# Weights staged in half-unit tiles, and two units split behind x at the end of the first PLE

## The chip, the cores and the metric

The program runs on 1 core of one Trainium2 chip. The metric is the device time of one execution in microseconds (us); the median of several executions is compared. One execution was also taken with the hardware profiler, and all rows below are of that one. The engines are PE (TensorE, matmuls), DVE (VectorE), ACT (ScalarE), POOL (GpSimd) and SP (SyncE, which here only issues DMAs). Each works through its own instructions in their order.

## The reference, cut to what matters

A decoder trunk of two layers over 256 tokens of width 1024, in float32:

```python
for i in range(2):
    x = layer_norm(a * x + 0.5 * swiglu(x, w_gate[i, 0], w_up[i, 0], w_down[i, 0]), ...)   # 2816 hidden columns
    mix = mixer_ab(x, ...) if i % 2 == 0 else mixer_cd(x, ...)      # [Mamba-2 SSD | S5], [HGRN2 | GLA]
    x = layer_norm(a * x + mix, ...)
    x = layer_norm(a * x + 0.5 * swiglu(x, w_gate[i, 1], w_up[i, 1], w_down[i, 1]), ...)
    x = x + sigmoid(x @ ple_w_gate[i]) * (p[i] @ ple_w_proj[i])     # "PLE"
```

The stages follow each other, in the kernel's names: f00 (the first SwiGLU), LN, ab, LN, f01, LN, PLE 0, f10, LN, cd, LN, f11, LN, PLE 1. Every matrix product reads all its weights from HBM once.

## The kernel before

**Weights.** All weights lie in one array `wall` of 189 units of [128, 2048] float32 (1 MB), in the order of use. `Weights.unit()` (lines 45 to 66) fetches the next one: SP issues its load (line 53) into a staging tile `wst_n`, of which the pool has two; then for each half j of 1024 columns ACT makes the rounded copy `wh_n_j` (line 61) and DVE the remainder `wl_n_j` = staged - `wh` (line 62). PE computes each product in three matmuls, x high with `wh`, x high with `wl`, and x low with `wh` (`mm3`). A staging tile is free for the next load once the DVE subtraction of its second half is done. `wh` and `wl` live in six half-unit buffers each, which is three units; the last two down units of a SwiGLU use a pool of their own.

**x.** `split_xT` (lines 105 to 114) does the same to x, which PE has transposed into PSUM (`tp_...`): ACT writes `xh` (line 112), DVE `xl` (line 113). It keeps both instructions as `g.anchors`. x is split in four pieces, token tile t (0, 1) by half c (0, 1) of its 1024 columns.

**Order.** A scheduler orders the instructions of each engine ahead of time, by times that it works out itself. `behind` adds an order to it: an instruction may not be placed ahead of given anchors on the same engine. `layer_norm` uses it: behind a layer norm the splits of units `at+1` and `at+2` (the second and third unit of the next stage) come after the splits of x of token tiles 0 and 1. `ple` (its `finish`, lines 291 to 312) makes the new x without such an order; its x is split at once for the next stage, f10, whose first units are 99, 100 and 101.

**A SwiGLU** has 11 blocks f of 256 hidden columns. A block's gate and up products take two units (`gu_f`, 48 matmuls of 512 columns), then `hidden` applies silu and the product (`sg`, ACT line 211, DVE line 212), PE transposes (`ht`), ACT and DVE split (`hh`, `hl`, line 218), and `down` takes one unit into the four accumulators `acc` (token tile by half, 24 matmuls). PE has matmuls of the next block between.

**S5 tables in f00.** Between the blocks of f00 the engines also build the tables of the S5 mixer, in eight parts b, and store them to HBM: DVE and ACT write `s5pk_b` (one buffer; lines 516, 530, 541), PE transposes `s5w_b_0`, `s5w_b_1` and multiplies `s5k_b`, ACT copies these into `s5pe` (one buffer; lines 553, 560, 565). POOL's queue stores them to `s5d` (line 543 for `s5pk`, line 566 for `s5pe`), so the next part's copies wait until the store has landed. In the middle POOL's queue also loads `s5m_1` (line 446), the input of parts 4 to 7.

Of the kernel before, what the change touches and what calls it, by code (L numbers as in the profile page):

```python
# [8 lines left out]
F32 = mybir.dt.float32  # L9
# [3 lines left out]
ALU = mybir.AluOpType  # L13
# [4 lines left out]
P = 128  # L18
# [15 lines left out]
def f32(ap):  # L34
    return ap.bitcast(F32)


class Weights:
# [6 lines left out]
    def unit(self, pool=None):  # L45
        g, nc = self.g, self.g.nc
        pool = pool or g.wsp
        n = self.at
        self.at += 1
        st = g.wst.tile([P, 2048], F32, tag="wst", name=f"wst_{n}")  # L50
        step = {0: 512, 1: 1024, 2: 1024}.get(n, 2048)
        for c in (slice(i, i + step) for i in range(0, 2048, step)):
            nc.sync.dma_start(st[:, c], self.wall[n][:, c])
        out = []
        for j in range(2):
            wh = pool.tile([P, 1024], F32R, tag="wh", name=f"wh_{n}_{j}")
            wl = pool.tile([P, 1024], F32R, tag="wl", name=f"wl_{n}_{j}")
            src = st[:, j * 1024:(j + 1) * 1024]
            step = 512 if n == 0 else 1024
            for c in (slice(i, i + step) for i in range(0, 1024, step)):  # L60
                ops = [nc.scalar.copy(wh[:, c], src[:, c])]  # L61
                ops.append(nc.vector.tensor_tensor(wl[:, c], src[:, c], f32(wh[:, c]), op=ALU.subtract))  # L62
                for op in ops:
                    behind(g, op, self.behind.get(n, ()))
            out.append((wh, wl))
        return out
# [40 lines left out]
def split_xT(g, t, half, src, xT):  # L107

    nc = g.nc
    s = slice(4 * half, 4 * half + 4)  # L110
    h, l = (x[:, s, t * P:(t + 1) * P] for x in xT)
    a = nc.scalar.copy(h, src)  # L112
    b = nc.vector.tensor_tensor(l, src, f32(h), op=ALU.subtract)
    g.anchors = a.ins, b.ins
# [165 lines left out]
def ple(g, i, pp, out):  # L280

    nc = g.nc
# [14 lines left out]
    def finish(t, c):  # L297
# [12 lines left out]
        for k in range(4):  # L310
            nc.tensor.transpose(tp[:, k, :], xn[t][:, (4 * c + k) * P:(4 * c + k + 1) * P], g.ident)
        split_xT(g, t, c, tp, xT)

    for kh in range(2):
        units[0][kh] = g.w.unit()
# [979 lines left out]
def tile_trunk(ctx: ExitStack, tc: tile.TileContext, xnat, xTd, pT, lnr, colsd, cstd, abrow, abdt, s5bc, cdlr, cdgu,  # L1295
               wall, out):
    nc = tc.nc
# [1 line left out]
    g.nc, g.tc = nc, tc  # L1299
    g.abrow, g.abdt, g.s5bc, g.cdlr, g.cdgu = abrow, abdt, s5bc, cdlr, cdgu  # L1300
    g.const = ctx.enter_context(tc.tile_pool(name="const", bufs=1))
    g.wst = ctx.enter_context(tc.tile_pool(name="wst", bufs=2))
    g.wsp = ctx.enter_context(tc.tile_pool(name="wsp", bufs=6))
    g.xp = ctx.enter_context(tc.tile_pool(name="xp", bufs=1))
    g.xt = ctx.enter_context(tc.tile_pool(name="xt", bufs=1))
# [224 lines left out]
```

## Time and profile before

| | |
|---|---|
| time, 3 runs | median 1233.27 us (1231.14 to 1238.06) |
| the profiled execution | 1235.71 us; its span (first to last instruction) 1233.9 us |
| busy in the span | PE 1204.1 us (98%), DVE 847.7 (69%), ACT 621.0 (50%), POOL 48.8 (4%) |
| DMA | 196 GB/s in the mean, 224.30 MB read from HBM |
| granted TensorE clock, mean | 0.996 of full speed |

Busy is the time in which an engine has an instruction in work. What the stages wait for is read from waits and timelines, whose rows give the start and length of an instruction and in brackets how long its engine stood idle before it and what released it. Matmul ends are modelled, so a matmul's spacing to the next is read rather than its length: a 128x512 matmul takes 0.39 us by itself and the next starts 0.23 us after it.

### The profile page before, as it was taken

How to read it: one execution, taken by the hardware profiler on the slowest of the kernel's cores; microseconds unless marked ns; L12 is line 12 of the kernel's file. 1: busy time of each engine (PE TensorE's matmuls, PEld its weight loads, DVE VectorE, ACT ScalarE, POOL GpSimd, SP SyncE). 2: the span in 40 equal slices, each digit the busy share in tenths (PEclk: the TensorE clock that was granted, in tenths of full speed). 3: DMA queues.
4: the chain of work that ended last, by engine and by line, in shares of the span. 5: the costliest groups of instructions: out<-in, count | busy, mean ns of one | idle time of the engine just before them, and what ended most of it. 6: DMA issues, size and time to landing. Idle time of an engine off the chain costs nothing.

```text
span 1233.9 us, 16226 instructions
## 1 busy us (share of the span) xinstructions
PE 1204.1 (98%) x6274; PEld 1011.5 (82%) x6274; DVE 847.7 (69%) x1353; ACT 621.0 (50%) x944; POOL 48.8 (4%) x78
## 2 busy tenths in 40 slices
PE   8999999899999999999999999999999999999998
PEld 6887788799997878888887888888888877888886
DVE  6997975679879866545568555546689876545466
ACT  5766765444535635444436443443575535444434
POOL 0000000020101000000000000000100110000000
PEclk9999999999999999999999999999999999999999
DMA  7676768687842646555546565554633327555532
GB/s 280 206 266 227 260 247 320 214 281 263 283 150 69 217 147 240 191 199 178 200 139 204 206 204 175 200 177 169 225 133 110 130 81 259 180 195 180 197 144 103
DMA packets 40797, 242.12 MB, mean 196 GB/s; under 512 B 4848, under 2 KB 5520, under 8 KB 17040
## 3 DMA queue, kind: packets, MB, share of 16 engines
q1 hardware_dynamic: 30672, 206.06, 48.7%
q0 software_dynamic: 3952, 18.88, 4.2%
q10 hardware_dynamic: 6096, 16.16, 3.9%
q8 instruction: 49, 0.80, 0.3%
q14 instruction: 28, 0.23, 0.1%
HBM read 224.30 MB, written 16.78 MB: 195 GB/s over the span
## 4 chain that ended last, share of the span: by engine, by line
PE 89%; DVE 4%; DMA 3%; ACT 2%; issue 1%; ACTq 0%; POOL 0%; DVEq 0%; POOLq 0%
PE gu_f L178 36%; PE acc_f L70 6%; PE acc_f L71 6%; PE acc_f L72 6%; PE pj_z L178 2%; PE ht_f L215 1%; PE acc_ple L71 1%; PE acc_ab L70 1%; PE acc_ab L72 1%; PE acc_ab L71 1%; PE acc_ple L70 1%; PE acc_ple L72 1%; PE s5v L689 1%; PE s5y L712 1%; PE pj_u L178 1%
## 5 line engine op out<-in xcount | busy, mean ns | idle before, releaser
L62 DVE TENSOR_TENSOR wl<-wst,wh 128x1024 fp32r<-128x1024 f32 (+1 forms) x378 | 453.4, 1216 | 255.9 <-ACT wh L61 249.9
L61 ACT CAST wh<-wst 128x1024 fp32r<-128x1024 f32 (+1 forms) x378 | 386.8, 1047 | 316.1 <-PE gu_f L178 102.8
L70 PE MATMUL acc_f<-wh,hh_f 128*128 128x512 f32 x352 | 138.3, 393 | 2.8 <-ACT hh_f L218 2.8
L71 PE MATMUL acc_f<-wl,hh_f 128*128 128x512 f32 x352 | 138.2, 393 | 0.0
L72 PE MATMUL acc_f<-wh,hl_f 128*128 128x512 f32 x352 | 136.1, 392 | 0.0
L70 PEld LDWEIGHTS acc_f<-wh,hh_f 128*128 128x128 f32 x352 | 66.5, 189 | 17.3 <-ACT hh_f L218 3.8
L178 PE MATMUL gu_f<-wh,xh_in 128*128 128x512 f32 x176 | 71.9, 414 | 6.0 <-ACT wh L61 6.0
L71 PEld LDWEIGHTS acc_f<-wl,hh_f 128*128 128x128 f32 x352 | 66.5, 189 | 13.6
L72 PEld LDWEIGHTS acc_f<-wh,hl_f 128*128 128x128 f32 x352 | 66.4, 189 | 13.7
L178 PE MATMUL gu_f<-wh,xh_ple 128*128 128x512 f32 x176 | 69.8, 397 | 1.4 <-ACT xh_ple L112 1.4
L178 PE MATMUL gu_f<-wl,xh_in 128*128 128x512 f32 x176 | 70.5, 404 | 0.0
L178 PE MATMUL gu_f<-wh,xh_ab 128*128 128x512 f32 x176 | 69.8, 396 | 0.5 <-ACT xh_ab L112 0.5
L178 PE MATMUL gu_f<-wl,xh_ab 128*128 128x512 f32 x176 | 68.9, 391 | 1.3 <-DVE wl L62 1.3
L178 PE MATMUL gu_f<-wh,xh_cd 128*128 128x512 f32 x176 | 69.9, 397 | 0.0
L178 PE MATMUL gu_f<-wl,xh_cd 128*128 128x512 f32 x176 | 68.9, 391 | 0.7 <-DVE wl L62 0.7
L211 ACT ACTIVATE sg_f<-gu_f 128x256 f32<-128x256 f32 x88 | 33.7, 383 | 71.2 <-PE gu_f L178 69.6
L178 PE MATMUL gu_f<-wl,xh_ple 128*128 128x512 f32 x176 | 68.7, 390 | 0.0
L178 PE MATMUL gu_f<-wh,xl_ab 128*128 128x512 f32 x176 | 66.9, 391 | 0.0
L178 PE MATMUL gu_f<-wh,xl_cd 128*128 128x512 f32 x176 | 66.8, 391 | 0.0
L178 PE MATMUL gu_f<-wh,xl_ple 128*128 128x512 f32 x176 | 66.7, 391 | 0.0
L178 PE MATMUL gu_f<-wh,xl_in 128*128 128x512 f32 x176 | 66.5, 393 | 0.0
L212 DVE TENSOR_TENSOR sg_f<-sg_f,gu_f 128x256 f32<-128x256 f32 x88 | 36.7, 417 | 29.3 <-ACT sg_f L211 29.3
(470 smaller groups left out, 2392.4 us busy)
## 6 DMA issues: line engine op xcount, KB each, us to landing
wst<-in_wall_dram SPq DMA_DIRECT2D x185, 1024.0 KB, 4.9
s5d<-s5pk POOLq DMA_DIRECT2D x8, 896.0 KB, 4.5
s5d<-s5pe POOLq DMA_DIRECT2D x8, 768.0 KB, 4.7
row<-in_lnr_dram SPq DMA_DIRECT2D x12, 512.0 KB, 6.7
W<-s5d ACTq DMA_DIRECT2D x8, 512.0 KB, 6.4
Q<-s5d ACTq DMA_DIRECT2D x8, 512.0 KB, 5.3
tab<-s5d ACTq DMA_DIRECT2D x8, 384.0 KB, 3.5
wst<-in_wall_dram SPq DMA_DIRECT2D x4, 512.0 KB, 6.4
```

The lines of the kernel that those rows point to most:

```text
L61: ops = [nc.scalar.copy(wh[:, c], src[:, c])]
L62: ops.append(nc.vector.tensor_tensor(wl[:, c], src[:, c], f32(wh[:, c]), op=ALU.subtract))
L70: nc.tensor.matmul(out, xh, wh, start=first, stop=False)
L71: nc.tensor.matmul(out, xh, wl, start=False, stop=False)
L72: nc.tensor.matmul(out, xl, wh, start=False, stop=last)
L178: nc.tensor.matmul(ps[t], x, w, start=kh == 0 and i == 0, stop=kh == 1 and i == len(mms) - 1)
L211: nc.scalar.activation(sg, ps[t][:, 0:256], AF.Silu)
L212: nc.vector.tensor_tensor(sg, sg, ps[t][:, 256:512], op=ALU.mult)
L215: nc.tensor.transpose(tp[:, k, :], sg[:, k * P:(k + 1) * P], g.ident)
L689: nc.tensor.matmul(v[:, i, q, :], W[:, i, q, :], U[:, NP * b + q, :], start=True, stop=True)
L712: nc.tensor.matmul(y[:, q, 1:64], Q[:, i, q, :], S[:, i, q, 0:63], start=False, stop=i == 1)
```

## The change

The staging tile is a half unit now: [128, 1024], with four in the pool instead of two whole ones. Each half has a load of its own, and its tile is free after its own subtraction. SP's order has 400 rows instead of 215, which is 185 loads more. In the last steps of PLE 0 (halves c = 1), `finish` records that the splits of unit 100 come behind the split of x of token tile 0, and those of unit 101 behind that of token tile 1. The last PLE returns before that line. In the changed file line 53 is line 57, lines 61 and 62 are 59 and 60, and lines 63 to 311 stand two lines lower in number.

```diff
--- before.py
+++ after.py
@@ -47,19 +47,17 @@
         pool = pool or g.wsp
         n = self.at
         self.at += 1
-        st = g.wst.tile([P, 2048], F32, tag="wst", name=f"wst_{n}")
-        step = {0: 512, 1: 1024, 2: 1024}.get(n, 2048)
-        for c in (slice(i, i + step) for i in range(0, 2048, step)):
-            nc.sync.dma_start(st[:, c], self.wall[n][:, c])
         out = []
         for j in range(2):
+            st = g.wst.tile([P, 1024], F32, tag="wst", name=f"wst_{n}_{j}")
             wh = pool.tile([P, 1024], F32R, tag="wh", name=f"wh_{n}_{j}")
             wl = pool.tile([P, 1024], F32R, tag="wl", name=f"wl_{n}_{j}")
-            src = st[:, j * 1024:(j + 1) * 1024]
             step = 512 if n == 0 else 1024
             for c in (slice(i, i + step) for i in range(0, 1024, step)):
-                ops = [nc.scalar.copy(wh[:, c], src[:, c])]
-                ops.append(nc.vector.tensor_tensor(wl[:, c], src[:, c], f32(wh[:, c]), op=ALU.subtract))
+                nc.sync.dma_start(st[:, c], self.wall[n][:, 1024 * j + c.start:1024 * j + c.stop])
+            for c in (slice(i, i + step) for i in range(0, 1024, step)):
+                ops = [nc.scalar.copy(wh[:, c], st[:, c])]
+                ops.append(nc.vector.tensor_tensor(wl[:, c], st[:, c], f32(wh[:, c]), op=ALU.subtract))
                 for op in ops:
                     behind(g, op, self.behind.get(n, ()))
             out.append((wh, wl))
@@ -310,6 +308,8 @@
         for k in range(4):
             nc.tensor.transpose(tp[:, k, :], xn[t][:, (4 * c + k) * P:(4 * c + k + 1) * P], g.ident)
         split_xT(g, t, c, tp, xT)
+        if c:
+            g.w.behind[g.w.at + 1 + t] = g.anchors
 
     for kh in range(2):
         units[0][kh] = g.w.unit()
@@ -1299,7 +1299,7 @@
     g.nc, g.tc = nc, tc
     g.abrow, g.abdt, g.s5bc, g.cdlr, g.cdgu = abrow, abdt, s5bc, cdlr, cdgu
     g.const = ctx.enter_context(tc.tile_pool(name="const", bufs=1))
-    g.wst = ctx.enter_context(tc.tile_pool(name="wst", bufs=2))
+    g.wst = ctx.enter_context(tc.tile_pool(name="wst", bufs=4))
     g.wsp = ctx.enter_context(tc.tile_pool(name="wsp", bufs=6))
     g.xp = ctx.enter_context(tc.tile_pool(name="xp", bufs=1))
     g.xt = ctx.enter_context(tc.tile_pool(name="xt", bufs=1))
```

The scheduler lays out all engines anew, so more moves than these lines say. Three places follow.

**ACT at the end of PLE 0**, from the splits of unit 100. `sg_ple0` is the gate of PLE, `xh_ple0` are the four pieces of the new x (token tile and half are the last two digits of the `tp_ple0` that it reads), 100 to 102 are units of f10. Before:

```order
L61 CAST wh_100_0_6265<-wst_100_6263 128x1024
L302 ACTIVATE sg_ple0_0_512_6190<-acc_ple0_0_1_6051 128x512
L61 CAST wh_100_1_6269<-wst_100_6263 128x1024
L61 CAST wh_101_0_6345<-wst_101_6343 128x1024
L112 CAST xh_ple0_6054<-tp_ple0_0_0_6128 128x4x128
L112 CAST xh_ple0_6054<-tp_ple0_1_0_6139 128x4x128
L302 ACTIVATE sg_ple0_1_512_6225<-acc_ple0_1_1_6053 128x512
L61 CAST wh_101_1_6349<-wst_101_6343 128x1024
L112 CAST xh_ple0_6054<-tp_ple0_0_1_6194 128x4x128
L61 CAST wh_102_0_6379<-wst_102_6377 128x1024
L61 CAST wh_102_1_6383<-wst_102_6377 128x1024
L112 CAST xh_ple0_6054<-tp_ple0_1_1_6229 128x4x128
```

Changed:

```order
L300 ACTIVATE sg_ple0_0_512_6385<-acc_ple0_0_1_6238 128x512
L110 CAST xh_ple0_6241<-tp_ple0_0_0_6319 128x4x128
L110 CAST xh_ple0_6241<-tp_ple0_1_0_6330 128x4x128
L300 ACTIVATE sg_ple0_1_512_6420<-acc_ple0_1_1_6240 128x512
L110 CAST xh_ple0_6241<-tp_ple0_0_1_6389 128x4x128
L59 CAST wh_100_0_6461<-wst_100_0_6460 128x1024
L59 CAST wh_100_1_6467<-wst_100_1_6466 128x1024
L110 CAST xh_ple0_6241<-tp_ple0_1_1_6424 128x4x128
L59 CAST wh_101_0_6543<-wst_101_0_6542 128x1024
L59 CAST wh_101_1_6549<-wst_101_1_6548 128x1024
L59 CAST wh_102_0_6579<-wst_102_0_6578 128x1024
L209 ACTIVATE sg_f10_0_0_6520<-gu_f10_0_0_6446 128x256
```

The first two pieces of x moved ahead of units 100 and 101; unit 100 is split behind the third piece and unit 101 behind the fourth. DVE's row has the same new order. PE's row is the same there up to the first five matmuls of unit 100.

**ACT in the middle of f00**, around unit 19, the down weights of block 5, and `hh_f00_5_0`, the hidden part that they meet. Before:

```order
L553 COPY s5pe_215<-s5w_2_0_1088 128x512
L492 ACTIVATE s5z_1_1321<-s5x_1_1319 128x256
L494 ACTIVATE s5z_1_1321<-s5z_1_1321 128x256
L553 COPY s5pe_215<-s5w_2_1_1094 128x512
L467 ACTIVATE s5e3_1_1310<-s5e3_1_1310 128x256
L61 CAST wh_19_0_1240<-wst_19_1238 128x1024
L61 CAST wh_19_1_1244<-wst_19_1238 128x1024
L560 COPY s5pe_215<-s5k_2_1100 96x4x32
L218 CAST hh_f00_5_0_1154<-ht_f00_5_0_1151 128x256
L565 COPY s5pe_215<-s5pe_215 32x4x32 x3
L530 ACTIVATE s5eb_4_1344<-s5e_4_1338,cs_209 128x32x16 x2
L541 COPY s5pk_4_1345<-s5sc_342 128x256
```

Changed (the copy of `s5w_2_0` stands right ahead of the first row, as the copy that waits for the store of `s5pe`):

```order
L467 ACTIVATE s5e3_1_1347<-s5e3_1_1347 128x256
L59 CAST wh_19_0_1274<-wst_19_0_1273 128x1024
L59 CAST wh_19_1_1280<-wst_19_1_1279 128x1024
L541 COPY s5pk_4_1382<-s5sc_349 128x256
L553 COPY s5pe_217<-s5w_2_1_1125 128x512
L560 COPY s5pe_217<-s5k_2_1131 96x4x32
L530 ACTIVATE s5eb_4_1381<-s5e_4_1375,cs_211 128x32x16 x2
L565 COPY s5pe_217<-s5pe_217 32x4x32 x6
L59 CAST wh_20_0_1424<-wst_20_0_1423 128x1024
L59 CAST wh_20_1_1430<-wst_20_1_1429 128x1024
L59 CAST wh_21_0_1460<-wst_21_0_1459 128x1024
L216 CAST hh_f00_5_0_1185<-ht_f00_5_0_1182 128x256
```

`s5pk_4`, all six small copies of `s5pe`, unit 20 and half of unit 21 now stand ahead of `hh_f00_5_0`. On PE the transposes `s5w_2_1` moved behind twelve more matmuls, and the four matmuls that read `hh_f00_5_1` follow directly on those of `hh_f00_5_0`. POOL's row at the same place, before:

```order
L542 MEMSET s5pk_3_1127 128x4
L566 DMA s5d1_88<-s5pe_215 128x1536
L446 DMA s5m_1_1146<-in_s5bc_dram 128x1024
L543 DMA s5d3_90<-s5pk_3_1127 128x1792
L542 MEMSET s5pk_4_1345 128x4
```

Changed:

```order
L542 MEMSET s5pk_3_1158 128x4
L446 DMA s5m_1_1177<-in_s5bc_dram 128x1024
L566 DMA s5d1_88<-s5pe_217 128x1536
L543 DMA s5d3_90<-s5pk_3_1158 128x1792
L542 MEMSET s5pk_4_1382 128x4
```

The load of `s5m_1` and the store of `s5pe` of part 1 changed places.

**ACT a block later**, ahead of the down matmuls of block 6 (`hh_f00_6`; unit 24 is a unit of block 8). Before:

```order
L61 CAST wh_23_1_1574<-wst_23_1568 128x1024
L530 ACTIVATE s5pk_5_1527<-s5q_5_1530,cs_209 128x32x16 x2
L218 CAST hh_f00_6_0_1370<-ht_f00_6_0_1367 128x256
L211 ACTIVATE sg_f00_7_0_1546<-gu_f00_7_0_1384 128x256
L61 CAST wh_24_0_1604<-wst_24_1602 128x1024
L218 CAST hh_f00_6_1_1380<-ht_f00_6_1_1377 128x256
L211 ACTIVATE sg_f00_7_1_1556<-gu_f00_7_1_1385 128x256
L61 CAST wh_24_1_1608<-wst_24_1602 128x1024
```

Changed:

```order
L59 CAST wh_23_1_1618<-wst_23_1_1617 128x1024
L216 CAST hh_f00_6_0_1407<-ht_f00_6_0_1404 128x256
L530 ACTIVATE s5pk_5_1570<-s5q_5_1573,cs_211 128x32x16 x2
L209 ACTIVATE sg_f00_7_0_1589<-gu_f00_7_0_1421 128x256
L216 CAST hh_f00_6_1_1417<-ht_f00_6_1_1414 128x256
L59 CAST wh_24_0_1648<-wst_24_0_1647 128x1024
L209 ACTIVATE sg_f00_7_1_1599<-gu_f00_7_1_1422 128x256
L59 CAST wh_24_1_1654<-wst_24_1_1653 128x1024
```

`hh_f00_6_0` is no longer behind `s5pk_5`, and `hh_f00_6_1` no longer behind unit 24. On PE the transposes that feed them (`ht_f00_6_0`, `ht_f00_6_1`) stand ten and eleven matmuls earlier.

## Rows read from the trace of the kernel before

**Rows 1.** The page, part 1: busy us (share of the span) and instructions of each engine

```profile
PE 1204.1 (98%) x6274; PEld 1011.5 (82%) x6274; DVE 847.7 (69%) x1353; ACT 621.0 (50%) x944; POOL 48.8 (4%) x78
```

**Rows 2.** Waits of PE: engine line <- releaser: us, times, longest us

```profile
PE acc_f L70 <- ACT hh_f L218: 2.8, 3, 1.3
```

**Rows 3.** Windows: us; busy PE, PEld, DVE, ACT, POOL; PEclk, DMA share, GB/s

```profile
480.00:640.00 160.00, 160.00 (x725) 132.16 (x724) 86.12 (x101) 70.23 (x96) 0.00 (x0) 1.00 0.57 195
...
150.00:153.40 3.40, 3.17 (x8) 2.49 (x9) 3.37 (x8) 1.40 (x3) 0.00 (x0) 0.50 1.05 310
```

**Rows 4.** Line 53, weight loads: issue ns min/median/max; then us to landing

```profile
L53 SPq DMA_DIRECT2D wst<-in_wall_dram x193: 327/328/433, 0.7 to 1211.9; - x193
...
DMA to landing us min/median/max: 3.8/4.9/9.3
```

**Rows 5.** Waits of SP's DMA queue: us, times, longest us

```profile
SPq L53 <- DVE wl L62: 648.0, 115, 33.3
```

**Rows 6.** Timeline of PE, end of PLE 0: start us, us, what, [idle before <-releaser]

```profile
670.61 1.03 PE L311 MATMUL tp_ple<-cs,x_ln 128*128 128x128 f32 x8
...
675.83 0.50 PE L178 MATMUL gu_f<-wh,xh_ple 128*128 128x512 f32 x1 [1.42 <-ACT xh_ple L112]
...
679.63 0.60 PE L311 MATMUL tp_ple<-cs,x_ln 128*128 128x128 f32 x4
...
682.28 0.48 PE L178 MATMUL gu_f<-wh,xh_ple 128*128 128x512 f32 x1
...
687.86 0.38 PE L215 MATMUL ht_f<-cs,sg_f 128*128 128x128 f32 x2
```

**Rows 7.** Timeline of ACT, the same stretch

```profile
674.25 1.04 ACT L61 CAST wh<-wst 128x1024 fp32r<-128x1024 f32 x1 [2.06 <-PE acc_ple L71]
...
675.20 1.07 ACT L112 CAST xh_ple<-tp_ple 128x512 fp32r<-128x512 f32 x2
...
680.27 0.59 ACT L112 CAST xh_ple<-tp_ple 128x512 fp32r<-128x512 f32 x1 [2.56 <-PE tp_ple L311]
...
685.66 0.39 ACT L211 ACTIVATE sg_f<-gu_f 128x256 f32<-128x256 f32 x1 [1.51 <-issue]
```

**Rows 8.** Timeline of POOL in f00 (spans are its issues)

```profile
105.33 0.53 POOL L566 DMA_DIRECT2D s5d<-s5pe  x1 [1.07 <-ACT s5pe L565]
...
105.89 0.54 POOL L446 DMA_DIRECT2D s5m<-in_s5bc_dram  x1
...
112.08 0.53 POOL L543 DMA_DIRECT2D s5d<-s5pk  x1 [5.66 <-DVE s5pk L516]
```

**Rows 9.** DMA issues from 100 to 125 us: count, KB each, median us to landing

```profile
s5d<-s5pk POOLq DMA_DIRECT2D x1, 896.0 KB, 8.6
...
s5m<-in_s5bc_dram POOLq DMA_DIRECT2D x1, 512.0 KB, 12.3
```

**Rows 10.** Timeline of ACT in f00

```profile
114.88 0.59 ACT L553 COPY s5pe<-s5w 128x512 f32<-128x512 f32 x1 [5.63 <-DMA s5d<-s5pe]
...
120.39 1.99 ACT L61 CAST wh<-wst 128x1024 fp32r<-128x1024 f32 x2
...
128.28 0.38 ACT L211 ACTIVATE sg_f<-gu_f 128x256 f32<-128x256 f32 x1
...
147.63 0.35 ACT L218 CAST hh_f<-ht_f 128x256 fp32r<-128x256 f32 x1
...
149.82 0.37 ACT L218 CAST hh_f<-ht_f 128x256 fp32r<-128x256 f32 x1
```

**Rows 11.** Timeline of PE in f00

```profile
115.52 0.66 PE L552 MATMUL s5w<-cs,s5eb 128*128 128x128 f32 x4 [1.74 <-ACT s5pe L553]
...
126.44 0.39 PE L70 MATMUL acc_f<-wh,hh_f 128*128 128x512 f32 x1
...
148.03 0.50 PE L70 MATMUL acc_f<-wh,hh_f 128*128 128x512 f32 x1 [1.30 <-ACT hh_f L218]
...
150.23 0.80 PE L70 MATMUL acc_f<-wh,hh_f 128*128 128x512 f32 x1 [1.01 <-ACT hh_f L218]
```

## The prediction

> **What bounds the kernel now.** I read the page's busy times first: PE is busy 1204.1 us of a span of 1233.9 us [rows 1]. Then the windows: in 160 us in the middle of f01 PE is busy for all 160.00 us, at full clock [rows 3]; two windows of the same length in f10 and f11 read the same. So the large SwiGLU stages wait for no weight, and nothing done to loads can shorten them. What is left is 29.8 us of PE idle time (span less busy): the start, the tail after the last matmul, and some 25 short waits where stages meet and in the middle of f00. Then the waits of PE, to see what ends them, and the timelines of those places. Two concern this change.
>
> At the end of PLE 0 the first matmul of f10 starts at 675.83 after 1.42 us idle, released by the copy of x, `xh_ple` [rows 6]. The transposes of those two pieces ran from 670.61 and took 1.03 us [rows 6], so the copies could have begun at about 671.6. They began at 675.20, because ACT works in order and had the split of unit 101 at 674.25 ahead of them, itself after 2.06 us idle [rows 7].
>
> In f00, `s5w` transposes wait 1.74 us at 115.52, and the down matmuls of block 6 wait 1.30 us at 148.03 and 1.01 us at 150.23 for their hidden part `hh_f` [rows 11], most of the 2.8 us that PE waits for `hh_f` [rows 2]. Right after these two waits the granted clock is 0.50, the 1.2 GHz level, from 150.0 to 153.4 [rows 3]: 3.4 us at half clock, which cost 1.7 us.
>
> **The change part by part.** *Half-unit loads in the steady stages: 0.* A SwiGLU block takes three units and 72 matmuls of 0.23 us, so 16.6 us; that is 2.8 us per half load. What a half load takes by itself no row shows. A whole one takes 4.9 us in the median and 3.8 us at least [rows 4], so a half takes between 1.9 us (half of the least) and 4.9 us (no shorter); I take the middle, 3.4 us. Four are in flight at once, so up to 11 us per half would still be hidden if they overlap. The work that hides it is PE's; without that cover each load's landing would show. The 185 added issues at 0.328 us [rows 4] are 61 us of SP's queue, which waited 648 us for free tiles [rows 5]. ACT's and DVE's splits are as many and as long as before.
>
> The Trainium skill speaks against this edit: "DMA: Bandwidth & Descriptors", section "Anatomy of one DMA", gives a fixed 2.0 us per transfer plus its bytes at 436 GB/s, and section "Bandwidth" says to batch to 1 MiB or more. By it a whole unit takes 4.4 us, where the trace has 4.9, and a half 3.2 us. By 3.2 us instead of 3.4 the last wait at PLE below would be 0.2 us shorter, and nothing else in the sum would move.
>
> *The splits behind x at the end of PLE 0: -0.1 us.* The two copies of x go ahead of units 100 and 101, so the 1.42 us wait goes. Then two things are later. First, unit 100 is split behind the third piece of x. Its transposes were at 679.63 for 0.60 us [rows 6]; 1.4 us earlier they end at 678.8, and then come the copy of x (0.59 us [rows 7]), the cast of `wh_100_0` (1.04 us, as at 674.25 [rows 7]) and the subtraction, which I take at 1.2 us, slightly above the cast. That ends at 681.6. PE reaches unit 100 at 682.28 - 1.4 = 680.9 [rows 6] and wants `wl_100_0` a matmul later, at 681.1: a new wait of 0.5 us. Second, the tile of that half comes free only at 681.6, so the first half of unit 102 loads then. It lands at 685.0 with 3.4 us. ACT casts it ahead of `sg_f10_0_0` and DVE subtracts it ahead of the product, so the hidden part of f10's first block follows: 685.0 + 1.05 cast + 1.2 subtraction + 0.4 product = 687.7. PE's transposes of it stood at 687.86 [rows 6] and would now be reached at 687.86 - 1.4 + 0.5 = 687.0: a new wait of 0.7 to 0.8 us. So -1.4 + 0.5 + 0.8 = -0.1. With 1.9 us for the load the last wait shrinks to about 0.4, because DVE is still at unit 101; with 4.9 us it is 2.3. Without the first new wait PE comes 0.5 us sooner and waits that much more, so the ends are -0.6 and +1.4.
>
> *The new order in f00: -1.0 us.* It has three steps.
>
> First, POOL. Before, the store of `s5pe` went at 105.33, the load of `s5m_1` at 105.89 and took 12.3 us to land, at 118.2; the store of `s5pk` went at 112.08 and took 8.6 us, landing at 120.7 [rows 8, 9]. The copy at 114.88 had waited 5.63 us for the first [rows 10]. With the first two swapped, the store of `s5pe` lands between 114.8 and 118.2. But `s5pk_4` needs the store of `s5pk_3`, which stays third and, the same bytes being ahead of it, lands near 120.7.
>
> Second, ACT. `s5pk_4` was late in the row; it is now right behind unit 19, and behind it stand one copy of `s5pe`, the other small ones, unit 20 and half of unit 21, and only then `hh_f00_5_0`. Before, ACT worked without a break from 120.39 to 128.28 [rows 10], 7.9 us, on the two casts of unit 19, `hh_f00_5_0` and the rest. The same list without `hh` (0.3) but with a copy of `s5pe` (0.5) and a cast (1.0) is 9.1 us, of which 2.0 is unit 19. If the store of `s5pe` lands at 118.2, unit 19 starts after a copy and an activation (0.5 + 0.4) at 119.1 and `hh` is free to start at 128.2; if it lands early, `s5pk_4` holds ACT to 120.7 and `hh` starts at 120.7 + 7.1 = 127.8. I take 128.0, done at 128.4. PE reached these matmuls at 126.44 [rows 11], including the 1.74 us wait, so it would be there at 124.7 and now wait about 3.7 us: +2.0 against before. If the stores land 2 us sooner it is 0.0; if ACT meets another 1 us of waiting, +3.0.
>
> Third, block 6. Its `hh_f00_6_0` and `hh_f00_6_1` ended at about 148.0 and 150.2 [rows 10], one behind `s5pk_5`, the other behind a cast of unit 24; both are now ahead of these, with their transposes ten matmuls (2.3 us) earlier. From block 5's to block 6's down matmuls PE needed 148.03 - 1.30 - 126.44 = 20.3 us [rows 11], so it comes at about 148.7. ACT has about 14 us of work in that time and must follow PE's transposes of S5 part 3 in it; I get `hh` some 2 us before it is wanted. So both waits go, -2.3, and the half clock after them, -1.7.
>
> Does the new 3.7 us wait bring a half clock of its own? At 115.52 a wait of 1.74 us did not; 2.3 us of waits within 3.2 us did [rows 3, 11]. I charge 1.0 of 1.7 us. The sum is +2.0 - 2.3 - 1.7 + 1.0 = -1.0; the ends are 0.0 - 4.0 = -4.0 and +3.0 - 4.0 + 1.7 + 1.3 (a wait left at block 6) = +2.0.
>
> *Everything else: 0.* At the layer norms' boundaries the order that ends the waits is the same in both programs; the start keeps its transfer sizes for units 0 to 2; the last PLE's final chain is unchanged. Other shifts in the mixers are by single groups that PE does not wait for; I allow 1 us either way.
>
> **The sum.** -1.0 - 0.1 = -1.1 us on the profiled 1235.7 us. That execution is 2.4 us above the median of 1233.3, so I forecast 1232.2 us.
>
> **The rivals.** *All waits go (faster).* If the stores land early enough for `hh_f00_5_0` to meet PE at 124.7, f00 gives 1.74 + 2.3 + 1.7 = 5.7 us, and if the load of unit 102 is short, PLE gives up to 1.4: 1226.2 us. For it: the moves at block 6 and PLE point that way. Against: `s5pk_4` must move ahead by over 3 us.
>
> *ACT held longer in f00 (slower).* The store that holds `s5pk_4` lands later than 120.7, since half loads now start sooner and share the same stretch. It decides from 1.0 us on: each us later is a us of PE. With 5 us the time is 1237; over 0.5% needs 7 us. For it: that stretch already stretches a 512 KB load to 12.3 us [rows 9]. Against: the bytes are the same.
>
> *Half loads run one behind another (slower).* Then a block takes 6 x 3.4 = 20.4 us instead of 16.6, and some 40 blocks add 150 us: about 1380 us. It decides from 2.8 us per half load on. Against it: the mean rate in f01 is 195 GB/s, with the DMA engines busy 0.57 of the time [rows 3], and before two whole loads could be in flight too. This is where the skill's rule on batching would lead; by its 3.2 us a block would take 19.2 us.
>
> *Nothing moves.* The waits only trade places: 1233. That lies inside the forecast's own range.
>
> **How the numbers follow.** 0.5% or 6.2 us is about what a measurement of this kernel can tell from no change. I give the forecast, within -4 to +3 us of the sum, 0.63; all waits gone 0.13; ACT held longer 0.20, of which 0.06 beyond 0.5%; loads in a row 0.04. So faster 0.13, same 0.77, slower 0.10. The range that leaves out 2 in 10 reaches from the case with all waits gone to ACT held 5 us and a little more: 1226.5 to 1238.0.
>
> **What would show it.** Right: `gu_f` at the start of f10 follows PLE's last matmul without a gap, then two waits of under 1 us, on DVE's `wl` and at `ht_f`; `hh_f00_5_0` ends near 128.4 with PE waiting for it; no wait at block 6; 160 of 160 us busy in f01. Wrong: a PE wait on `wh` or `wl` in a steady block, a `s5pk` store that lands far from 120.7, a half clock at a place not named here, or a wait in the mixers, which the sum takes at nothing.

## The result, and the profile after

The changed kernel takes 1248.16 us in the median of four runs (1241.10 to 1249.94), the kernel before 1233.89 us in the median of its four (1231.14 to 1238.06): a ratio of 1.0102, 95% interval 1.0053 to 1.0151. This ratio is not the quotient of the two medians, which is 1.0116. The medians lie 14.3 us apart, where I had forecast 1232.2 and had put 0.10 on slower. A second measurement of the same program (e12 below) gave 1.0090, interval 1.0067 to 1.0113. The profiled execution took 1249.18 us, with a span of 1247.4 us, 13.5 more than before.

Part 1 of the page after answers to [rows 1]: busy us and share.

```profile
PE 1213.0 (97%) x6274; PEld 1019.2 (82%) x6274; DVE 850.4 (68%) x1353; ACT 622.9 (50%) x945; POOL 50.6 (4%) x78
```

PE does the same 6274 matmuls and is busy 8.9 us longer. Work that takes longer with the same instructions points to the clock, so the windows come next (columns as in [rows 3]):

```profile
480.00:640.00 160.00, 160.00 (x726) 132.14 (x725) 87.24 (x101) 73.99 (x101) 0.00 (x0) 1.00 0.63 202
...
226.00:232.80 6.80, 5.27 (x12) 4.13 (x13) 6.05 (x11) 4.25 (x5) 0.93 (x1) 0.50 0.85 286
267.00:273.80 6.80, 6.26 (x29) 6.30 (x30) 2.58 (x6) 1.29 (x2) 2.90 (x4) 0.51 0.66 182
877.90:881.30 3.40, 3.40 (x12) 2.74 (x11) 0.91 (x2) 0.59 (x1) 0.21 (x1) 0.50 0.93 320
946.00:952.80 6.80, 6.80 (x23) 5.60 (x22) 5.43 (x10) 3.98 (x7) 0.00 (x0) 0.51 0.07 28
...
150.00:153.40 3.40, 3.40 (x18) 2.81 (x18) 3.40 (x8) 0.59 (x1) 0.00 (x0) 1.00 1.01 353
```

The steady stretch of f01 still reads 160 of 160 us: no block waits for a half load. The clock drop at 150 of [rows 3] is gone. But four stretches now run at 0.50, the 1.2 GHz level, 23.8 us in all, and a fifth of some 3 us lies behind 1024. Before, there were two of 3.4 us each, at 150 and at 228; the first of the four lies where the second of these was. Each microsecond at half clock does half a microsecond of work, so that is at most some 10 of the 13.5 us, and the 8.9 us of longer busy time is the part that fell on work. PE's waits, beside [rows 2], say what stands ahead of them:

```profile
PE acc_f L68 <- ACT hh_f L216: 3.0, 2, 2.5
PE s5v L689 <- DMA U<-udram: 2.9, 1, 2.9
...
PE s5y L712 <- DVE S L700: 1.3, 1, 1.3
...
PE ht_f L213 <- DVE sg_f L210: 1.0, 1, 1.0
```

Three of the four are new: `s5v` and `s5y`, both in the ab mixer, and `ht_f` behind PLE 0. The wait at `s5y` is not in the profile of e12 below, which is the same program. Two more, of 0.83 us in f00 and 1.80 us behind it, come up in the account of the prediction. The loads, beside [rows 4] and [rows 5]:

```profile
L57 SPq DMA_DIRECT2D wst<-in_wall_dram x378: 327/328/650, 0.7 to 1224.9; - x189
...
DMA to landing us min/median/max: 3.4/4.6/11.9
```

```profile
SPq L57 <- DVE wl L60: 659.6, 245, 21.6
```

A half takes 4.6 us to land where I took 3.4, nearly as long as a whole unit's 4.9. SP waits as long as before for free tiles.

**Where the time went.** I compare the start of the same matmul in the two traces: the first transpose behind f00 (`tp_ln`, 226.44 before), the first matmul of PLE 0 (`acc_ple`, 650.81), the first of cd (`pj_hq`, 863.19) and the last matmul of PLE 1's gate (1228.76). The differences, split by these marks, for all kernels of this study (us against the profile of before; the ratio is the one on record for each kernel's runs against those of the kernel before beside them, and differs from the quotient of the medians by up to 0.002):

| kernel | f00 | LN, ab, f01 | PLE 0, f10 | cd to end | sum | ratio, 95% interval |
|---|---|---|---|---|---|---|
| changed | -2.0 | +9.4 | +0.9 | +4.7 | +13.1 | 1.0102 [1.0053, 1.0151] |
| e12 changed again | -1.4 | +8.2 | +1.1 | -0.2 | +7.8 | 1.0090 [1.0067, 1.0113] |
| e1 half tiles only | -0.9 | +8.6 | -1.0 | +1.5 | +8.4 | 1.0077 [1.0053, 1.0100] |
| e2 PLE order only | -1.8 | +1.3 | -0.3 | -0.1 | -0.9 | 0.9981 [0.9961, 1.0001] |
| e3 two loads, whole tile | -4.4 | +0.1 | -0.4 | +3.4 | -1.2 | 0.9965 [0.9947, 0.9983] |
| e4 changed, uT first | -1.6 | +2.6 | +1.0 | +1.5 | +3.6 | 1.0035 [1.0016, 1.0053] |
| e8 e4 less PLE order | -1.7 | +2.0 | -1.0 | -0.1 | -0.8 | 1.0017 [0.9998, 1.0035] |
| e11 e4, Silu first | -1.8 | +1.7 | -0.3 | +2.8 | +2.4 | 1.0029 [1.0012, 1.0047] |
| e10 changed, s5v later | -0.7 | +2.2 | +1.0 | -0.4 | +2.2 | 1.0033 [1.0018, 1.0048] |
| e5 before, uT late | -2.0 | +0.1 | +0.4 | 0.0 | -1.5 | 1.0008 [0.9985, 1.0031] |
| e9 e5, s5v early | -0.7 | +6.1 | +0.1 | -0.1 | +5.5 | 1.0064 [1.0043, 1.0086] |
| e6 e3, PLE order, uT first | -4.3 | +1.2 | +3.7 | -1.4 | -0.8 | 1.0007 [0.9991, 1.0023] |
| e7 before, 8.2 us added | -0.2 | +7.5 | +1.6 | +1.4 | +10.2 | 1.0088 [1.0058, 1.0118] |

One profile has the clock drops of its own execution, so a sum can differ from the ratio by a few us; the columns of stages where no clock drop differs are steadier. How much a column moves by the execution alone can be read in f00: e2, e5, e7 and e9 have there the order of matmuls and splits of the kernel before, instruction for instruction, and read -1.8, -2.0, -0.2 and -0.7. One of the twelve runs of e2, slow at 1250.45 us and a mean clock of 0.985, is left out of its ratio.

**The ab mixer** holds most of it. Its S5 half needs u. ACT and DVE each copy half of it into `uT` (lines 655 and 657), POOL's queue stores `uT` to HBM (line 664, `udram`) and, when that has landed, loads it in four pieces into `U` (line 668), which PE's `s5v` matmuls read. In the changed program the copies stand behind more weight splits. DVE there, with the numbers of the units, before:

```
L62 TENSOR_TENSOR wl_36_1<-wst_36,wh_36_1 128x1024
L655 COPY uT_0<-ct_u0_1 128x512
L62 TENSOR_TENSOR wl_37_0<-wst_37,wh_37_0 128x1024
```

and changed:

```
L60 TENSOR_TENSOR wl_36_1<-wst_36_1,wh_36_1 128x1024
L60 TENSOR_TENSOR wl_37_0<-wst_37_0,wh_37_0 128x1024
L60 TENSOR_TENSOR wl_37_1<-wst_37_1,wh_37_1 128x1024
L60 TENSOR_TENSOR wl_38_0<-wst_38_0,wh_38_0 128x1024
L655 COPY uT_0<-ct_u0_1 128x512
```

The timelines of DVE, POOL and PE of the kernel before in that stretch (POOL's spans are its issues):

```profile
246.70 0.69 DVE L655 COPY uT<-ct_u 128x512 f32<-128x512 f32 x1 [1.91 <-PE ct_u L620]
...
248.47 0.59 POOL L664 DMA_DIRECT2D udram<-uT  x1 [14.46 <-ACT uT L657]
252.53 2.95 POOL L668 DMA_DIRECT2D U<-udram  x4 [3.48 <-PE pc_u L590]
...
263.68 1.89 PE L689 MATMUL s5v<-U,W 128*128 128x64 f32 x16
```

and of the changed kernel:

```profile
250.04 0.68 DVE L655 COPY uT<-ct_u 128x512 f32<-128x512 f32 x1
...
251.26 0.59 POOL L664 DMA_DIRECT2D udram<-uT  x1 [18.39 <-ACT uT L657]
258.39 2.94 POOL L668 DMA_DIRECT2D U<-udram  x4 [6.54 <-PE pc_bc L591]
...
267.54 3.65 PE L689 MATMUL s5v<-U,W 128*128 128x64 f32 x16 [2.90 <-DMA U<-udram]
```

The copy is 3.3 us later, the store is issued 2.8 us later, and from its issue to that of the loads it is 7.1 us instead of 4.1, so the loads are issued 5.9 us later. The last of them lands at 267.29 instead of 262.55. The slack was small: before, PE reached `s5v` 1.1 us after the last load had landed. It now waits 2.90 us, and the window from 267.0 shows the matmuls behind the wait at half clock; 16 `s5v` matmuls take 3.65 us instead of 1.89.

### The profile page after: what moved, and what is told of

Its sections match the earlier page's. It is cut to its first block, busy times and chain, and to the rows that moved or that the text cites. A ratio compares the mean times of both kernels' runs of the same rounds, so it can differ in the third digit from the quotient of the medians.

```text
span 1247.4 us, 16836 instructions
## 1 busy us (share of the span) xinstructions
PE 1213.0 (97%) x6274; PEld 1019.2 (82%) x6274; DVE 850.4 (68%) x1353; ACT 622.9 (50%) x945; POOL 50.6 (4%) x78
## 4 chain that ended last, share of the span: by engine, by line
PE 70%; issue 5%; DVE 3%; DMA 2%; ACT 1%; POOL 0%; ACTq 0%; DVEq 0%; POOLq 0%
PE gu_f L176 28%; PE acc_f L70 5%; PE acc_f L69 5%; PE acc_f L68 5%; PE acc_ple L69 1%; PE acc_ab L68 1%; PE acc_ab L69 1%; PE acc_ab L70 1%; PE ht_f L213 1%; PE acc_ple L68 1%; PE acc_ple L70 1%; PE pj_u L176 1%; PE pj_hg L176 1%; PE pj_gv L176 1%; PE lv_h L1149 1%
## 5 line engine op out<-in xcount | busy, mean ns | idle before, releaser
L68 PE MATMUL acc_f<-wh,hh_f 128*128 128x512 f32 x352 | 134.7, 391 | 3.0 <-ACT hh_f L216 3.0
```

Of the source, the lines that this page charges most:

```text
L68: nc.tensor.matmul(out, xh, wh, start=first, stop=False)
```

## The experiments

Theory A: the late copies of `uT` cost the ab stage its 7 us, by PE's wait and the clock drop behind it. The rivals are the order at PLE (B), the half loads that crowd the store (C, in e5 and e9), and transfers of half the size that cost by themselves (D). (In the expectation of e1, C stands for a clock that differs from run to run, and in that of e4, D for the crowding.) Diffs are against the kernel that is named; `...` marks what is left out.

**e1, half tiles without the PLE order** (against changed):

```diff
         split_xT(g, t, c, tp, xT)
-        if c:
-            g.w.behind[g.w.at + 1 + t] = g.anchors
```

> The half-unit tiles alone, without the order at the end of PLE 0. Up to PLE 0 every engine's order is that of the changed kernel. Theory A (the loss sits in the ab stage: the first copy of u for S5 is laid behind three more splits, its store to HBM starts 2.8 us later, PE waits 2.9 us for U and the clock halves for 6.8 us after it): the wait on U shows again, between 2 and 4 us, and the time is that of the changed kernel less about 1 us, 1240 to 1248. Rival B (the loss comes from the order at the end of PLE 0): no loss here, 1230 to 1236. Rival C (the loss is only granted clock that differs from run to run): the time follows the clock, about 1241 at 0.995 and 1248 at 0.989.

Measured: 1244.65 us, ratio 1.0077 [1.0053, 1.0100], a wait of 3.45 us at `s5v` and half clock from 268 to 275. The loss is there without the PLE order. Nor is it the clock of single runs: the wait stands in the profiles of the changed kernel, of this one and of e12 (2.90, 3.45 and 3.40 us).

**e2, the PLE order with whole units** (against before): the two lines that e1 takes out are put in.

> The order at the end of PLE 0 alone, on whole-unit tiles. Up to PLE 0 every engine's order is that of the kernel before. Theory A: as the kernel before within 2 us (1.4 us of the wait for x gone, and up to 2 us lost again since unit 102 is loaded later and as a whole), 1232 to 1236. Rival B: the whole loss, 1245 or more.

Measured: 1234.82 us, ratio 0.9981 [0.9961, 1.0001]. The waits at PLE are 0.45 and 0.36 us instead of 1.42, and the stage gains 0.3 us. So B falls as well.

**e3, whole staging tiles filled by two loads of 512 KB each** (against before):

```diff
-        step = {0: 512, 1: 1024, 2: 1024}.get(n, 2048)
+        step = 512 if n == 0 else 1024
         for c in (slice(i, i + step) for i in range(0, 2048, step)):
             nc.sync.dma_start(st[:, c], self.wall[n][:, c])
```

> Whole-unit tiles as before, but each filled by two loads of 512 KB; a tile is still freed as a whole. On DVE the first copy of u stands behind one split more than before (three more in the changed kernel). Theory A: U lands later than before by 1 to 2 us, so PE's wait on it is under 1 us, and the time is 1233 to 1238. Rival D (smaller transfers are slower in themselves, wherever the work stands): PE waits for U as long as in the changed kernel, or waits on weights appear, and the time is 1240 or more.

Measured: 1229.66 us, ratio 0.9965 [0.9947, 0.9983], the fastest kernel here, and faster than theory A had it. The loads by size and number are those of the changed kernel and land as its loads do:

```profile
L53 SPq DMA_DIRECT2D wst<-in_wall_dram x378: 327/374/1647, 0.7 to 1211.0; - x189
...
DMA to landing us min/median/max: 3.3/4.5/11.2
```

So D falls. The Trainium skill, "DMA: Bandwidth & Descriptors", section "Bandwidth", asks for batches of 1 MiB or more; halving these 1 MB loads did not slow the kernel. In the steady blocks PE waits for no load in either form, so there was nothing to lose. The gain shows in f00: -4.4 us here and -4.2 in e6, where the kernels with the order of before read 0 to -2.0. The scheduler laid out f00 anew here too, so whether the earlier halves or the new order bring it is not shown.

**e4, changed, with the copies of uT first** (against changed): the splits of units 37 and 38 may not stand ahead of the two copies.

```diff
+    kept = []
     def keep(h, ps):
...
+        kept.append(copy(by_step(uT[:, k, :]), ps.rearrange("p k (c s) -> p k s c", s=4)).ins)
...
         channel_tiles(g, pool, f"u{c}", keep)
+        g.w.behind[g.w.at + 2] = g.w.behind[g.w.at + 3] = tuple(kept)
```

> The changed kernel with the splits of units 37 and 38 laid behind the first copies of u, as they stood before. Theory A: the store of u starts near 248.5 again, U lands near 263, PE's wait of 2.9 us and the 6.8 us at half clock after it are gone: 5 to 7 us less than the changed kernel at the same clock elsewhere, 1236 to 1243. Rival D (the half loads crowd the stores and loads of u whatever the order): the store still takes 6 us and U lands after 266, and nothing is won.

Measured: 1239.28 us, ratio 1.0035 [1.0016, 1.0053]; no wait for U, no half clock there, and LN to f01 costs 2.6 us instead of 8.2 to 9.4. What is left sits at PLE (+1.0) and in cd.

**e8, e4 without the PLE order.**

> e4_uT_first (1239.28) without the PLE order: half-unit tiles, splits of units 37 and 38 behind the uT copies. If the PLE order is what costs e4_uT_first its 2 us between the PLE and the third FFN: offset there 0 to +0.5 instead of +2, median 1236.5 to 1238, ratio 1.001 to 1.003. If the half tiles cost it by themselves: offset +2 again, median 1238.5 to 1240.5, ratio 1.003 to 1.005.

Measured: 1237.49 us, ratio 1.0017 [0.9998, 1.0035]. The kernel differs from e1 in the place of the uT copies alone (on DVE this is the only move, on ACT and PE a few rows around it moved too), and takes 7.2 us less (1244.65). POOL and PE of its profile:

```profile
248.01 0.59 POOL L663 DMA_DIRECT2D udram<-uT  x1 [14.90 <-ACT wh L59]
252.31 2.95 POOL L667 DMA_DIRECT2D U<-udram  x4 [3.72 <-PE pc_u L588]
...
264.61 1.89 PE L688 MATMUL s5v<-U,W 128*128 128x64 f32 x16
```

With half loads all around it, it is 4.3 us from the issue of the store to that of the loads, and `s5v` does not wait.

**e5, before, with the copies of uT as late as in the changed kernel** (against before): the opposite of e4, in whole units.

```diff
+                for ins in self.ahead.get((n, j), ()):
+                    behind(g, ins, [op.ins for op in ops])
             out.append((wh, wl))
...
         channel_tiles(g, pool, f"u{c}", keep)
+        g.w.ahead[g.w.at + 2, 0] = kept[:1]
+        g.w.ahead[g.w.at + 3, 0] = kept[1:]
```

> The kernel before, whole units, with one edit: the two copies of the S5 input uT stand behind the splits of weight units 37 and 38 on ACT and DVE, where the changed kernel has them (DVE behind three splits, ACT behind two). Theory A (the late copy is what costs the ab stage): the store of uT issues some 2.8 us later than the 248.47 of before, the U loads land some 2.8 us later than 262.55, which is 1.7 us past the 263.68 at which PE asked for them, so a wait of 1.5 to 3.5 us at the S5 matmuls and a stretch of half clock behind it: ab longer by 4 to 8 us, median 1238 to 1243, ratio 1.003 to 1.007. Rival C (the smaller transfers crowd the store; the copy's place alone costs nothing): no wait over 0.5 us there, ratio 0.998 to 1.002.

Measured: 1235.52 us, ratio 1.0008 [0.9985, 1.0031]: no loss, as rival C had it. But PE's row shows that more had moved than the edit says: the scheduler knew of the late U and put 40 matmuls of `pc_bc0_1` (0.12 us each) ahead of `s5v`, where before had 9.

```profile
250.92 0.59 POOL L669 DMA_DIRECT2D udram<-uT  x1 [18.90 <-ACT uT L660]
255.31 2.95 POOL L673 DMA_DIRECT2D U<-udram  x4 [3.81 <-DMA udram<-uT]
...
265.47 1.89 PE L694 MATMUL s5v<-U,W 128*128 128x64 f32 x16
```

PE comes to `s5v` 3.8 us later than the 2.0 us gained in f00 would have it, with its time filled. The run did not tell A from C; the next two do.

**e9, e5 with s5v held at its old place on PE** (against e5):

```diff
-                nc.tensor.matmul(ps[:, j, :], wh[:, k, :], xh[:, k, :], start=k == 0, stop=False)
+                op = nc.tensor.matmul(ps[:, j, :], wh[:, k, :], xh[:, k, :], start=k == 0, stop=False)
+                if (name, h, j, k) in (("bc0", 1, 0, 3), ("bc1", 0, 0, 0)):
+                    behind(g, op, g.s5v)
...
```

> e5_uT_late (whole units, late uT copies, 1235.52) with one edit: the S5 matmuls of the first batch keep the place on PE that they have in the kernel before (behind 9 matmuls of pc_bc0_1, where e5_uT_late had 40), so that no other work stands between the late U and PE. Theory A (the copies' lateness, where PE has nothing put in between, is enough for the loss, without half tiles): U lands near 264.8 as in e5_uT_late, PE asks for it near 261.8, wait 2.5 to 3.5 us and a stretch of half clock behind it, median 1239 to 1244, ratio 1.003 to 1.007. Rival C (it takes the half tiles' transfers): wait under 1 us, ratio 0.998 to 1.002.

Measured: 1242.05 us, ratio 1.0064 [1.0043, 1.0086], with whole units and whole loads:

```profile
252.04 0.59 POOL L671 DMA_DIRECT2D udram<-uT  x1 [18.71 <-ACT uT L662]
...
266.22 3.65 PE L696 MATMUL s5v<-U,W 128*128 128x64 f32 x16 [3.06 <-DMA U<-udram]
```

```profile
265.50:272.30 6.80, 6.08 (x28) 6.11 (x29) 2.62 (x7) 0.56 (x1) 2.90 (x4) 0.50 0.85 263
```

A wait of 3.06 us, 6.8 us at half clock, and a stage 6.1 us longer: the wait and 3.1 us of clock behind it. The late copy is enough; half tiles aren't needed. More of ab's order moved than the edit names, so it is the wait and the stretch behind it, more than the total, that show this. The Trainium skill tells of such a pair in "TensorE: Matmul & The Clock Gate", section "HAM oscillation — how this bites in real kernels": in a kernel there, a wait for a DMA lets the clock fall, and the work behind it starts cold, which is at the lower clock. The trace agrees: a wait of 3.06 us, and half clock for the work behind it.

**e10, changed, with s5v later on PE** (against changed): behind 39 matmuls of `pc_bc0_1` instead of 17.

```diff
...
+                if (name, h, j, k) == ("bc0", 1, 1, 4):
+                    behind(g, g.s5v, [op.ins])
...
```

> The changed kernel with one edit: PE does the S5 matmuls of the first batch behind 39 matmuls of pc_bc0_1 instead of 17; U comes as late as before the edit. 22 matmuls at some 0.11 us put 2.5 us of work over the wait of 2.90. Theory A (PE's wait and the half clock behind it are the price): wait under 0.7 us, no half clock at 267 to 274, ab shorter by 5 to 7 us than in the changed kernel, median 1240 to 1243, ratio 1.004 to 1.007. If the late U costs further on in any case: the offset behind ab stays at +7, ratio 1.009 or more.

Measured: 1238.62 us, ratio 1.0033 [1.0018, 1.0048], somewhat less than theory A had. U is as late as in the changed kernel (its loads are issued at 261.94), but nothing waits, and the clock stays up:

```profile
268.76 1.89 PE L691 MATMUL s5v<-U,W 128*128 128x64 f32 x16
```

```profile
265.50:276.00 10.50, 10.50 (x89) 10.34 (x88) 9.48 (x16) 6.05 (x8) 2.90 (x4) 1.00 0.94 269
```

LN to f01 costs 2.2 us instead of 8.2 (e12). So the price is PE's wait and its clock, not a late U in itself.

**e12, the changed kernel again.**

> The changed kernel itself, with more runs and on the chip of the three kernels beside it: ratio 1.007 to 1.012, with the wait for U (2.9 us) and half clock behind it again. If the first measurement was high by the clock of its few runs: 1.004 to 1.007.

Measured: 1243.96 us, ratio 1.0090 [1.0067, 1.0113]; a wait of 3.40 us at `s5v` and half clock from 267.7 to 274.5. In its profile the drops in cd are missing, and cd to the end costs -0.2 us instead of +4.7.

**e11, e4 with the first Silu of f10 ahead of unit 102** (against e4), for what is left at PLE:

```diff
...
+            if (name, f, t) == ("f10", 0, 0):
+                g.w.behind[g.w.at + 1] = tuple(op.ins for op in ops)
```

> e4_uT_first (1239.28) with the splits of unit 102 held behind the first Silu and its product in the FFN after the PLE, so that ACT and DVE have there the order of e2_behind_x. If the displaced Silu is what costs e4_uT_first its wait of 1.14 us at 689.81 and its +2 us: wait gone, offset 0 at that FFN's end, median 1236 to 1238, ratio 1.000 to 1.003. If the half tiles' loads set it: the wait stays at another instruction, ratio 1.003 to 1.005.

Measured: 1238.68 us, ratio 1.0029 [1.0012, 1.0047]. The wait at `ht_f` is gone and PLE to f10 goes from +1.0 to -0.3, as foretold. The total does not show it: the ratio can't be told from e4's 1.0035, and the median lies a little above the range foreseen. The one profile has 6.8 us at half clock in cd, where that of e4 has 3.4:

```profile
936.00:942.80 6.80, 6.80 (x21) 5.54 (x20) 5.73 (x10) 4.36 (x7) 0.00 (x0) 0.50 0.02 8
```

**e6, e3 with the PLE order and the uT copies first**, the candidate for the best kernel.

> The candidate for the best: whole-unit tiles, each filled by two 512 KB loads (as in e3_two_loads, 1229.66), with the PLE order of the change, and the splits of units 37 and 38 held behind the uT copies. If the gains add (theory A, with e2_behind_x's -0.3 us): 1228.0 to 1230.5, ratio 0.994 to 0.998, no wait for U. If the PLE order costs with these loads what it does in e4_uT_first (+2 us up to the next FFN): 1230.5 to 1233, ratio 0.997 to 1.000.

Measured: 1236.06 us, ratio 1.0007 [0.9991, 1.0023], against 0.9965 for e3, and slower than both sides had it. At PLE, PE and the clock behind it:

```profile
686.90 0.69 PE L215 MATMUL ht_f<-cs,sg_f 128*128 128x128 f32 x2 [2.25 <-DVE sg_f L212]
```

```profile
687.00:690.40 3.40, 3.40 (x10) 2.78 (x11) 3.40 (x5) 2.05 (x3) 0.00 (x0) 0.53 0.48 128
```

The same displaced Silu as in the changed kernel, here with a clock drop: +3.7 us. In e3 the two half loads alone had left only 0.45 us of the wait at PLE, so there was nothing for the order to gain.

**e7, before, with 36 superfluous matmuls in f01** (8.2 us without a gap; their sums are started afresh afterwards, so this kernel does more work than the others), to see whether the drops in cd come with PE's time of arrival:

```diff
...
+        for i in range(pad if kh == 0 else 0):
+            part(kh, 0, pieces, True)
         for t in range(NT):
             part(kh, t, pieces)
...
```

> The kernel before, with work added: in the second FFN's block 5, 36 matmuls that are done once more than needed (their sums are started afresh afterwards), 36 x 0.227 us = 8.2 us with PE never idle. All that follows comes 8.2 us later, as in the changed kernel; nothing else moves. Theory P (whether a stretch of the mixer cd at 940 to 953 us is granted half clock goes by when PE comes to it, not by the weights' tiles): half clock of 3 to 7 us there, median 1245 to 1249 (before + 8.2 + 2 to 5). Rival Q (it goes by the half tiles and the order around them): no half clock there, as in the profile of before, and median 1242.5 to 1244.5.

Measured: 1245.26 us, 9.8 more than before, of which the work is 8.2. The profile has a wait of 3.05 us at PLE instead of 1.42, which neither side had foreseen, and in cd, where the profile of before has none, a stretch at half clock in which PE never pauses:

```profile
945.90:949.30 3.40, 3.40 (x10) 2.79 (x11) 3.40 (x7) 2.88 (x5) 0.00 (x0) 0.50 0.25 104
```

So such a drop comes without any change to the weights, and e3, with whole tiles, has one in cd too. That it is the time of arrival which decides isn't shown: 9.8 us less the 8.2 of work and the 1.6 of the longer wait leaves nothing for the clock in the median. So the profile speaks for theory P and the median for rival Q.

## Why the prediction was wrong

**The steady stages: right.** 160 of 160 us busy. A half load takes 4.6 us, not 3.4, inside the 1.9 to 4.9 that I had given it. The 3.2 us that the prediction works out from the Trainium skill ("DMA: Bandwidth & Descriptors", section "Anatomy of one DMA — SWDGE (gpsimd) path") come from a formula which that section gives for the path of DMAs issued by GpSimd. The weight loads here are issued by SP.

**f00: the waits came much as foretold, the gain is not shown.** I had -1.0 and bounds of -4 and +2; the column reads -2.0 here and -1.4 in e12. PE after, beside [rows 11], and ACT, beside [rows 10]:

```profile
127.98 0.50 PE L68 MATMUL acc_f<-wh,hh_f 128*128 128x512 f32 x1 [2.55 <-ACT hh_f L216]
...
188.32 0.50 PE L176 MATMUL gu_f<-wh,xh_in 128*128 128x512 f32 x1 [0.83 <-DVE sg_f L210]
```

```profile
120.56 0.41 ACT L541 COPY s5pk<-s5sc 128x256 f32<-128x256 f32 x1 [1.51 <-DMA s5d<-s5pk]
...
127.57 0.36 ACT L216 CAST hh_f<-ht_f 128x256 fp32r<-128x256 f32 x1
```

`s5pk_4` did wait for the store of `s5pk_3` until 120.56 (I had 120.7) and `hh_f00_5_0` ended at 127.93 (128.4). The wait is 2.55 where I had 3.7, and the waits at block 6 are gone, as foretold. The wait of 0.83 at 188.32, which all seven profiles of half tiles have, was not in my sum.

The term that fails here is the clock's. I had counted 1.7 us for the half clock behind the waits at block 6. But e2 has the order of before in f00, and PE's rows and the window show the same two waits with no drop behind them:

```profile
147.31 0.50 PE L70 MATMUL acc_f<-wh,hh_f 128*128 128x512 f32 x1 [1.29 <-ACT hh_f L218]
...
149.70 0.50 PE L70 MATMUL acc_f<-wh,hh_f 128*128 128x512 f32 x1 [1.20 <-ACT hh_f L218]
```

```profile
147.00:153.40 6.40, 4.89 (x21) 3.53 (x22) 6.37 (x14) 3.20 (x8) 0.53 (x1) 1.00 0.93 325
```

The profiles of e5 and e9, with the same order, show the same. The drop of [rows 3] belonged to that one execution. The half clock that I had charged behind the new wait is no steadier: it is missing in this profile and stands in that of e12, from 127.8. Without the clock, the waits named here are 3.4 us after (2.55 + 0.83) and 4.1 before (1.74 + 1.30 + 1.01), a gain of 0.7. The column reads -0.7 to -2.0 in the seven profiles of half tiles and 0 to -2.0 in the five with the f00 of before, so it shows no gain, and that it lies inside my bounds says little.

**PLE: right in kind, mis-sized.** I had -1.4 + 0.5 + 0.8 = -0.1; it is +0.9. PE, beside [rows 6], and ACT, beside [rows 7]:

```profile
682.30 0.50 PE L176 MATMUL gu_f<-wh,xh_ple 128*128 128x512 f32 x1 [0.45 <-ACT xh_ple L110]
...
689.56 0.50 PE L176 MATMUL gu_f<-wl,xh_ple 128*128 128x512 f32 x1 [0.36 <-DVE wl L60]
696.10 0.44 PE L213 MATMUL ht_f<-cs,sg_f 128*128 128x128 f32 x2 [1.02 <-DVE sg_f L210]
```

```profile
693.41 1.05 ACT L59 CAST wh<-wst 128x1024 fp32r<-128x1024 f32 x1 [1.83 <-DMA wst<-in_wall_dram]
694.36 0.38 ACT L209 ACTIVATE sg_f<-gu_f 128x256 f32<-128x256 f32 x1
```

The wait at the first matmul does not go, 0.45 is left; the wait on `wl` is 0.36; and the Silu stands behind a cast that waits for its load, as I had said, which makes PE wait 1.02 at `ht_f`. These waits are 1.83 us against 1.42 before, so +0.4; no wait shows the other 0.5. (By its own terms the low end that I gave is -0.5, not -0.6.) With the order, half tiles cost +1.0 there (e4); with the Silu first -0.3 (e11); without the order -1.0 (e8). So the half loads alone gave what the order was to give, and in half tiles the order loses 2.0 us.

**The step that failed is "*Everything else: 0.*"** I had allowed 1 us either way for "single groups that PE does not wait for" in the mixers. The copy of `uT` is such a group, PE does not wait for it, but for the store and the loads that follow from it, and their slack was 1.1 us before. I had looked at what PE waited for in the trace of before, where this chain doesn't appear because it was just in time, and not at what has little slack. In the changed program the loads of U are issued 5.9 us later, and that costs the wait of 2.9 to 3.4 us and as much again by the clock (e9: 6.1; e8 against e1: 7.2). Of the 5.9 us the place of the copy explains some 2.8; the other 3.0 are the store, which took 6.08 us to land instead of 3.37. In whole units, as late, it took 3.7 (e5, e9), in half tiles, not late, 3.3 (e8); it is slow only where both meet, and the weight loads issued at 250.15, 251.88 and 254.38 stand beside it. The Trainium skill says in "DMA: Bandwidth & Descriptors", section "Issuing engines are not separate DMA queues", that DMAs of all issuing engines run on the same 16 engines and interleave; that fits, but half loads stand beside the store in e8 as well (249.28 and 250.41), where it took 3.3 us. So what slowed the store stays open.

**None of the rivals was it.** ACT held longer in f00 did not happen, the loads did not run one behind another, and the time was none of the four. The prediction's last part names the right sign, "a half clock at a place not named here, or a wait in the mixers", without a chance for it.

**The clock was in the sum for f00 alone.** Some 9 to 10 of the 13.5 us of the profiled pair are half clock. Part stands at waits: ab, and the layer norm behind f00, where `pj_u` waits 1.80 us instead of 0.86 and the stretch at half clock is 6.8 us instead of 3.4. The failed step had this boundary at nothing too: the wait is 1.64 to 1.80 us in all seven profiles of half tiles and 0.80 to 0.96 in the five with the f00 of before. The longer stretch is not the half tiles' alone, for e2, with whole units, has 6.8 us there with a wait of 0.96. Part does not hang on waits: the last wait of PE ahead of the drop at 946 is one of 0.24 us at 882.

**What stays open.** With both causes taken out (e8, e11) the half tiles stand at 1.0017 and 1.0029, e3 at 0.9965. In the profiles they differ from e3 in f00 (2.6 us for e8) and in ab (1.8 us); which of the moved instructions makes that was not taken apart.

## What to carry to other kernels

When a change gives a scheduler new freedom, compare the orders around every store that is read back, and list these chains with their slack, not only the waits: what is just in time shows no wait until it is late. If a chain has come late, either its first copy is put ahead of work that can wait (e4), or its reader is put behind work that PE has anyway (e10); both gave back most of it. Where only an earlier start of the first half is wanted, two loads into one whole tile were the fastest kernel here (0.9965), without a change of the tile. And a stretch at half clock in one profile is no term for a sum until another execution of the same order has it too.

## What the runs showed of the hardware

The granted clock falls to 0.50 in stretches of 3.4 or 6.8 us, and not only behind waits. Nor does a wait decide by itself: at `hh_f00_5_0` PE waited 2.55 us in the changed kernel and the clock held, and 2.23 us in e12, the same program, and it fell. The timeline of PE in the changed kernel, in cd:

```profile
944.32 0.64 PE L1149 MATMUL lv_g<-X_g 64*124 64x64 f32 x4
944.89 2.53 PE L1149 MATMUL lv_h<-X_h 128*127 128x64 f32 x16
947.35 1.09 PE L1149 MATMUL lv_g<-X_g 64*124 64x64 f32 x4
948.37 0.79 PE L176 MATMUL pj_hg<-wh,xl_f 128*128 128x512 f32 x1
```

There is no idle time ahead of any of these; the last wait of PE before them is at 882. The 16 `lv_h` matmuls take 1.99 us in the profile of before, and 2.53 here since the clock falls among them; then 512-column matmuls follow each other by 0.43 us instead of 0.23 until 952.8. What PE did ahead of the drop was a run of `lv_g` and `lv_h` matmuls. This part of cd ran at full clock in the profiles of before, e2, e5, e6, e8, e9, e10 and e12, and had a stretch at half in those of changed, e1, e3, e4, e7 and e11. What decides stayed unknown, and runs of one kernel differ with the clock: e11 took 1233.94 us in a run with a mean clock of 0.997, and 1242.48 in one with 0.992.
